# MLPs of a two-layer trunk, first product, chunks 5 to 8: block products accumulated in PSUM, front products adjacent, and A12 by B21 in halves from chunk 6 on

## The chip, the cores and the metric

One core of a Trainium2 chip runs the whole program. The metric is the device time of one execution in microseconds (us), here the median of three runs. PE is TensorE (matmuls), PEld its weight loads, DVE is VectorE, ACT is ScalarE, POOL is GpSimd; SP is the engine whose queue issues nearly all DMAs of this kernel. Every engine works through its own instructions strictly in the order in which they stand in the program, and waits on semaphores for the others.

## The reference

A trunk of two layers on 1024 tokens of width 1024 in float32. Each layer has a mixer, an MLP and a gated projection of a side input p. The change touches the MLPs only:

```python
hn = rms_norm(h, ln_mlp[layer])
h = h + jnp.square(jax.nn.relu(hn @ w_mlp1[layer])) @ w_mlp2[layer]
gate = jax.nn.sigmoid(rms_norm(h, ln_ple[layer]) @ w_ple_gate[layer])
h = h + (p[layer] @ w_ple_proj[layer]) * gate
```

w_mlp1 is 1024 x 4096, w_mlp2 is 4096 x 1024. The "first product" is hn @ w_mlp1.

## The kernel before

**Precision.** Every float32 operand is split into a high part (ACT copies it to the type fp32r) and a low part (DVE subtracts), and mm3 makes three matmuls of each pair: high by high, high by low, low by high.

**The first product** is computed transposed, hidden features on the partitions, in NCH = 8 chunks of 512 hidden features (the code counts them 0 to 7, the text 1 to 8). Each chunk is a 2 x 2 block product (A the weights, B the normed activations, split by 512 of the contraction and by 512 tokens) and is done after Strassen and Winograd with seven block products in place of eight. A block product (product, L335) has two output tiles of 128 x 512, one PSUM bank each, and 24 matmuls of 512 columns. front (L419) makes the first two, A11 by B11 and A12 by B21, accumulated in one pair of banks: after the first ACT copies the running value out as u, after the second it makes g11 = relu^2. rest (L432) makes the other five: (A11-A21) by T3, copied out as v; S1-A11 by T2, added to u, and u to v, on DVE; A22 by T4, on top of the first in its banks, giving g21; S1 by T1, giving g22; and (A12-S2) by B22, on top of that, giving g12. T1 to T4 are sums of the activations' blocks. After each, DVE adds what is in PSUM to u or v, and ACT takes relu and square.

**Halves.** From chunk 3 on (HALVED) the last of these, A12-S2 by B22, is itself done with seven products of half size (halved, L375): 42 matmuls of 256 columns in place of 24 of 512. Their activation parts are made once (halves, L355) and held in the buffers of the pool tmp (tag t, four buffers) and two others. p16 and p57 are two further PSUM banks for its sums.

**Results.** Seven arrays are saved to DRAM per chunk (save, L410), the second product's own operands: gd[0] from g12, gd[1] g22, gd[2] g21, gd[3] and gd[4] from g22 and g21 less v, gd[5] from v = g11 + g12, and gd[6] g21 - g11.

**The second product** follows at once (product2, L570), seven products of 16 steps; each step loads a tile of such an array (graw), splits it, and gives PE 12 matmuls of 512 columns. Its weights come through tiles keep and raw. Early on, split_p (L649) loads p in four tiles through the pool tmp, transposes them on DVE and splits them.

**Buffers and order.** The tiles of the region have one buffer each, named by tag: u of chunk c lies in c0, c1 or c2, c3 (even or odd c), g11 in c4, c5 or c6, c7, g12, g21, g22 in c8 to c13. v lies in two buffers of the pool small. The second product's raw tiles go round c0, c1, c4, c5, its split tiles round c2, c6, c8, c10 and their neighbours, except the first four, which take the buffers of B21:

```python
raws, ring = itertools.cycle((0, 1, 4, 5)), itertools.cycle((2, 6, 8, 10))
```

A tile's next writer waits until its last reader is done, a save's DMA included. The weights' blocks go through 8 raw buffers and 12 split ones. PSUM has 8 banks, four tags with two each, taken in turn (mm_ps, L164). Fronts run two chunks ahead of their rests (those of chunks 3 and 4 are kept in DRAM meanwhile). The code is written in this order, but the order in which an engine's instructions stand is decided by the framework's scheduler, which places them by its own timeline. Each DMA of SP signals one of eight semaphores in turn, and waits until the DMA before it on the same semaphore has landed.

## Time and profile before

| | us |
|---|---|
| median of 3 runs | 2466.21 (2464.63 to 2469.31) |
| the profiled execution | 2463.99 |
| its span, first to last instruction | 2462.3 |
| first save of a chunk, MLP 1 and MLP 2 | 535.1 and 1803.1 |
| last save of a chunk, MLP 1 and MLP 2 | 794.3 and 2058.6 |

The profile is one execution on the chip. A row of the timeline has the start, the length, the engine, the line of the program, the operation, output <- input by the program's names, and how many such instructions stand in a row; a bracket at the end is the engine's idle time before it and what ended that. A row of groups has the count, the busy time, the mean length in ns, and the idle time before. Matmuls overlap in the pipeline, so a matmul's length is more than the time from one start to the next. For DMAs, the time to landing is from the issue on the queue to the semaphore's update. In the lines of this profile, L226 and L225 are split, L284 is tt, L324 is load, L412 is save, L658 the transpose of p.

### The profile page before, as it was taken

How to read it: one execution, taken by the hardware profiler on the slowest of the kernel's cores; microseconds unless marked ns; L12 is line 12 of the kernel's file. 1: busy time of each engine (PE TensorE's matmuls, PEld its weight loads, DVE VectorE, ACT ScalarE, POOL GpSimd, SP SyncE). 2: the span in 40 equal slices, each digit the busy share in tenths (PEclk: the TensorE clock that was granted, in tenths of full speed). 3: DMA queues.
4: the chain of work that ended last, by engine and by line, in shares of the span. 5: the costliest groups of instructions: out<-in, count | busy, mean ns of one | idle time of the engine just before them, and what ended most of it. 6: DMA issues, size and time to landing. Idle time of an engine off the chain costs nothing.

```text
span 2462.3 us, 40587 instructions
## 1 busy us (share of the span) xinstructions
PE 2446.6 (99%) x13709; PEld 2105.3 (85%) x13709; DVE 1922.5 (78%) x3806; ACT 1332.3 (54%) x2740; POOL 319.2 (13%) x304
## 2 busy tenths in 40 slices
PE   9999999999999999999999999999999999999999
PEld 7898998888888888888899999988878888888887
DVE  7787766699788888566568888876898788978677
ACT  6554474465555434454366766664655555445543
POOL 0221231000000000000244443342000000000010
PEclk9999999999999999999999999999999999999999
DMA  8385654456557856553347766787456559657772
GB/s 249 114 260 119 172 186 153 141 168 210 190 173 262 269 182 200 186 174 112 116 104 167 163 166 161 195 225 239 141 172 222 178 183 308 227 184 223 231 246 86
DMA packets 555032, 459.12 MB, mean 186 GB/s; under 512 B 248260, under 2 KB 416456, under 8 KB 554824
## 3 DMA queue, kind: packets, MB, share of 16 engines
q1 hardware_dynamic: 524472, 451.28, 59.5%
q10 hardware_dynamic: 29584, 3.68, 1.0%
q8 instruction: 108, 1.77, 0.3%
q0 software_dynamic: 768, 1.57, 0.2%
q14 instruction: 100, 0.82, 0.1%
HBM read 322.04 MB, written 134.37 MB: 185 GB/s over the span
## 4 chain that ended last, share of the span: by engine, by line
PE 94%; DVE 2%; ACT 2%; DMA 2%; issue 1%; POOL 0%; SPq 0%; DVEq 0%; ACTq 0%; POOLq 0%
PE mm L79 83%; PE po L79 3%; PE qk L79 2%; PE aux L79 2%; PE tr L82 1%; DMA a_dram<-lg 0%; DVE w L226 0%; PE aux L82 0%; PE pvn L79 0%; PE pkq L79 0%; PE pst L79 0%; DMA raw<-in_w_mlp_dram 0%; PE pks L79 0%; ACT guv L1697 0%; ACT w L225 0%
## 5 line engine op out<-in xcount | busy, mean ns | idle before, releaser
L79 PE MATMUL mm<-g,w 128*128 128x512 f32 x2592 | 602.9, 394 | 0.4 <-DVE g L226 0.4
L225 ACT CAST w<-raw 128x512 fp32r<-128x512 f32 (+1 forms) x622 | 377.6, 613 | 414.0 <-PE mm L79 339.2
L79 PEld LDWEIGHTS mm<-g,w 128*128 128x128 f32 x2592 | 486.8, 188 | 114.5 <-DVE g L226 0.8
L79 PE MATMUL mm<-hi,w 128*128 128x512 f32 (+1 forms) x1728 | 528.4, 383 | 0.4 <-DVE w L226 0.4
L79 PE MATMUL mm<-w,hi 128*128 128x256 f32 (+2 forms) x2528 | 500.5, 294 | 0.2
L226 DVE TENSOR_TENSOR w<-raw,w 128x512 fp32r<-128x512 f32 (+2 forms) x534 | 362.6, 685 | 128.0 <-ACT w L225 119.9
L79 PEld LDWEIGHTS mm<-w,hi 128*128 128x128 f32 x2528 | 400.4, 188 | 14.1 <-DVE w L226 0.4
L79 PEld LDWEIGHTS mm<-hi,w 128*128 128x128 f32 x1728 | 316.6, 188 | 63.9 <-DVE w L226 0.8
L79 PE MATMUL mm<-w,lo 128*128 128x256 f32 (+2 forms) x1264 | 367.8, 292 | 0.0
L79 PE MATMUL mm<-lo,w 128*128 128x512 f32 (+1 forms) x864 | 329.2, 382 | 0.0
L79 PE MATMUL mm<-t,w 128*128 128x512 f32 x1152 | 274.0, 394 | 0.4 <-DVE t L226 0.2
L79 PEld LDWEIGHTS mm<-t,w 128*128 128x128 f32 x1152 | 216.1, 188 | 51.8 <-DVE t L226 1.1
L79 PEld LDWEIGHTS mm<-w,lo 128*128 128x128 f32 x1264 | 237.6, 188 | 5.4
L79 PEld LDWEIGHTS mm<-lo,w 128*128 128x128 f32 x864 | 162.8, 188 | 31.9
L225 ACT CAST g<-graw 128x512 fp32r<-128x512 f32 x216 | 132.6, 617 | 33.0 <-DMA graw<-gd 25.3
L226 DVE TENSOR_TENSOR g<-graw,g 128x512 fp32r<-128x512 f32 x216 | 147.5, 686 | 3.7 <-ACT g L225 3.6
L1134 ACT ACTIVATE lg<-lg,nm 128x128 f32<-128x128 f32 (+7 forms) x128 | 99.2, 775 | 74.7 <-DVE nm L1131 72.8
L266 POOL TENSOR_TENSOR r<-ms,mhalf 128x4 f32<-128x4 f32 x12 | 12.5, 1043 | 940.4 <-DVE ms L264 914.1
L226 POOL TENSOR_TENSOR w<-raw,w 128x512 fp32r<-128x512 f32 (+1 forms) x88 | 113.7, 1313 | 132.1 <-ACT w L225 98.9
L350 ACT ACTIVATE g<-g 128x512 f32<-128x512 f32 x96 | 60.2, 630 | 64.7 <-DVE g L284 64.6
L1131 DVE CUSTOM_DVE_ANT_0 lg<-qk,al 128x512 f32<-128x512 f32 (+3 forms) x128 | 72.3, 568 | 25.7 <-PE qk L79 22.4
L79 PE MATMUL mm<-ohi,w 128*128 128x512 f32 x256 | 85.9, 400 | 0.2 <-DVE aT L1348 0.2
(353 smaller groups left out, 3689.7 us busy)
## 6 DMA issues: line engine op xcount, KB each, us to landing
raw<-in_w_mlp_dram SPq DMA_DIRECT2D x352, 256.0 KB, 3.3
graw<-gd SPq DMA_DIRECT2D x224, 256.0 KB, 2.8
gd<-g SPq DMA_DIRECT2D x192, 256.0 KB, 3.2
raw<-in_w_ple_gate_dram SPq DMA_DIRECT2D x76, 256.0 KB, 3.7
acc<-h_dram SPq DMA_DIRECT2D x64, 256.0 KB, 4.3
keep<-in_w_mlp_dram SPq DMA_DIRECT2D x64, 256.0 KB, 5.1
raw<-in_w_in_e_dram SPq DMA_DIRECT2D x60, 256.0 KB, 3.7
h_dram<-acc SPq DMA_DIRECT2D x48, 256.0 KB, 2.2
```

The source lines that it names most:

```text
L79: self._next(self.engine.matmul(*a, **k))
L82: self._next(self.engine.transpose(*a, **k))
L225: self.nc.scalar.copy(hi, src)
L226: (lo_engine or self.nc.vector).tensor_tensor(lo, src, f32(hi), ALU.subtract)
L266: nc.gpsimd.tensor_tensor(r, ms, self.mhalf[:, 0:4], ALU.pow)
L350: nc.scalar.activation(g, src, AF.Relu)
L1131: nc.vector.tensor_tensor_reduce(out=lg[:, k0:k1], in0=ps[:, : k1 - k0], in1=al[:, u0 + k0 : u0 + k1], scale=-1.0, scalar=3.0e38 if c == 0 ...
L1134: nc.scalar.activation(lg[:, :n], lg[:, :n], AF.Exp, bias=nm[:, r, nch - 1 : nch], scale=-1.0, accum_out=me.sums[:, b, r : r + 1])
```

## The change

Chunks 5 to 8 (CHAINED = 4, counted from 0) go through a new function, chain, in place of front and rest:

- A11 by B11 is made in a pair of banks and copied out by ACT as g11. A12 by B21 goes into banks of its own (ps2), and DVE adds it to g11. Then S1-A11 by T2, (A11-A21) by T3 and A22 by T4 follow in the first pair of banks, one on top of another; ACT copies u out after the first, g22 after the second, and after the third g21 is made straight from PSUM. S1 by T1 and (A12-S2) by B22 go on as before.
- The front products of a chunk stand right ahead of its other products, not two chunks earlier.
- All four chunks use c0, c1 for u, c4, c5 for g11, c8, c9 for g12, c10, c11 for g21, and the two buffers of v for g22; u is overwritten with g11 + g12 and saved. The last subtractions and the saves of gd[3] and gd[4] move into the next chunk (close), behind its A12 by B21.
- In chunk 5 halves is called for B21 too (ys2, kept in c2, c3, c6, c7, c12, c13 and in B21's own buffers), and from chunk 6 on A12 by B21 is done by halved: 42 matmuls of 256 columns in place of 24 of 512.

```diff
@@ -27,6 +27,7 @@
 RB = 8
 AHEAD = 7
 HALVED = 2
+CHAINED = 4
 WB = 12
 EARLY = 3000
 LAG = 3
@@ -352,28 +353,37 @@
 
         L, R = slice(0, 256), slice(256, 512)
 
-        def halves():
-
-            y = {(1, 1): [[z[:, L] for z in b22[k]] for k in (0, 1)], (2, 1): [[z[:, L] for z in b22[k]] for k in (2, 3)],
-                 (2, 2): [[z[:, R] for z in b22[k]] for k in (2, 3)], 1: [[z[:, R] for z in b22[k]] for k in (0, 1)]}
-            y2, y3 = ([self.tp.tile([P, 2, 256], F32R, tag="t", name=self.nm("y")) for _ in range(2)] for _ in range(2))
-            y4 = [self.sp.tile([P, 2, 256], F32R, tag=t, name=self.nm("y"), bufs=1) for t in ("sqs1", "rb1")]
-            y.update({n: [[z[:, k] for z in parts] for k in range(2)] for n, parts in ((2, y2), (3, y3), (4, y4))})
+        def halves(b, spare):
+
+            y = {(1, 1): [[z[:, L] for z in b[k]] for k in (0, 1)], (2, 1): [[z[:, L] for z in b[k]] for k in (2, 3)],
+                 (2, 2): [[z[:, R] for z in b[k]] for k in (2, 3)], 1: [[z[:, R] for z in b[k]] for k in (0, 1)]}
+            parts = spare()
+            y.update({n: [[z[:, k] for z in parts[n]] for k in range(2)] for n in parts})
             for k in range(2):
                 d, e = (self.raw(1, HT)[:, 0] for _ in range(2))
-                tt(d, *(f32(z) for z in b22[k]), ALU.add)
-                tt(e, *(f32(z) for z in b22[2 + k]), ALU.add)
+                tt(d, *(f32(z) for z in b[k]), ALU.add)
+                tt(e, *(f32(z) for z in b[2 + k]), ALU.add)
                 tt(d[:, L], d[:, R], d[:, L], ALU.subtract)
                 tt(d[:, R], e[:, R], d[:, R], ALU.subtract)
                 tt(e[:, R], e[:, R], d[:, L], ALU.subtract)
                 tt(e[:, L], e[:, L], e[:, R], ALU.subtract)
                 self.split(d[:, L], *y[1][k])
-                for src, parts in ((e[:, R], y2), (d[:, R], y3), (e[:, L], y4)):
-                    self.split(src, *(z[:, k] for z in parts))
+                for src, n in ((e[:, R], 2), (d[:, R], 3), (e[:, L], 4)):
+                    self.split(src, *(z[:, k] for z in parts[n]))
                 yield y
 
+        def small():
+            y = {n: [self.tp.tile([P, 2, 256], F32R, tag="t", name=self.nm("y")) for _ in range(2)] for n in (2, 3)}
+            y[4] = [self.sp.tile([P, 2, 256], F32R, tag=t, name=self.nm("y"), bufs=1) for t in ("sqs1", "rb1")]
+            return y
+
+        def freed():
+            return {n: [self.slot(f"c{o + i}", [P, 2, 256], F32R, "y") for i in range(2)] for n, o in ((2, 2), (3, 6), (4, 12))}
+
         def halved(raws, y, ps, u):
 
+            new = not ps
+            ps = ps or [self.mm_ps() for _ in range(2)]
             a0, a1 = raws
             lo, hi = slice(0, P), slice(P, 2 * P)
             s12, s4 = self.raw(2, 256), self.raw(2, P)
@@ -392,8 +402,8 @@
             u0, u1 = u
             sub(p16, a0, lo, y[1, 1], True)
             tt(u0[:, L], u0[:, L], p16, ALU.add)
-            sub(ps[0][:, L], a1, lo, y[2, 1])
-            sub(ps[1][:, L], a1, hi, y[4])
+            sub(ps[0][:, L], a1, lo, y[2, 1], new)
+            sub(ps[1][:, L], a1, hi, y[4], new)
             sub(p5, s12, lo, y[1], True)
             for z in u:
                 tt(z[:, R], z[:, R], p5, ALU.add)
@@ -401,11 +411,12 @@
             sub(p7, a0, hi, y[3], True)
             u1 = u1.rearrange("p (h t) -> p h t", h=2)
             tt(u1, u1, p7.unsqueeze(1).to_broadcast([P, 2, 256]), ALU.add)
-            sub(ps[0][:, R], s4, slice(0, P), y[2, 2])
+            sub(ps[0][:, R], s4, slice(0, P), y[2, 2], new)
             sub(p16, s12, hi, y[2])
             tt(u0[:, R], u0[:, R], p16, ALU.add)
             tt(u1, u1, p16.unsqueeze(1).to_broadcast([P, 2, 256]), ALU.add)
             marks.append(self.pe.mark)
+            return ps
 
         def save(n, c, g):
             for i in range(2):
@@ -450,7 +461,7 @@
                 tt(u[i], u[i], ps6[i], ALU.add)
                 tt(v[i], u[i], v[i], ALU.add)
             if c == HALVED:
-                made = halves()
+                made = halves(b22, small)
                 next(made)
             product(a22, t4, ps)
             for i in range(2):
@@ -487,6 +498,74 @@
                 tt(g21[i], g21[i], v[i], ALU.subtract)
             save(4, c, g22)
             save(5, c, g21)
+
+
+        def chain(c, close):
+
+            u, g11, g12, g21 = (tiles((f"c{o}", f"c{o + 1}"), "g") for o in (0, 4, 8, 10))
+            g22 = [self.sp.tile([P, HT], F32, tag=f"{n}0", name=self.nm("v"), bufs=1) for n in ("sqs", "rb")]
+            ps = product(block(c, 0, 0), b11)
+            for i in range(2):
+                nc.scalar.copy(g11[i], ps[i])
+            a12 = block(c, 0, 1)
+            if c > CHAINED:
+                ps2 = halved(a12, ys2, None, g11)
+            else:
+                ps2 = product(a12, b21)
+            close()
+            s1 = self.slot("B", [P, 2, 2, 256], F32, "s1")
+            s1 = [s1[:, i] for i in range(2)]
+            a21, a22, a11 = block(c, 1, 0), block(c, 1, 1), block(c, 0, 0)
+            for i in range(2):
+                tt(s1[i], a21[i], a22[i], ALU.add)
+                tt(a21[i], a11[i], a21[i], ALU.subtract)
+                tt(a11[i], s1[i], a11[i], ALU.subtract)
+            for i in range(2):
+                cols = L if i and c > CHAINED else slice(0, HT)
+                tt(g11[i][:, cols], g11[i][:, cols], ps2[i][:, cols], ALU.add)
+                relu2(g11[i], g11[i])
+            product(a11, t2, ps)
+            for i in range(2):
+                nc.scalar.copy(u[i], ps[i])
+            if c == CHAINED:
+                made = halves(b21, freed)
+                next(made)
+            product(a21, t3, ps)
+            for i in range(2):
+                nc.scalar.copy(g22[i], ps[i])
+            if c == CHAINED:
+                ys2.update(next(made))
+            product(a22, t4, ps)
+            for i in range(2):
+                relu2(g21[i], ps[i])
+                tt(g11[i], g21[i], g11[i], ALU.subtract)
+            save(3, c, g21)
+            save(7, c, g11)
+            ps = product(s1, t1)
+            for i in range(2):
+                tt(g22[i], g22[i], ps[i], ALU.add)
+                relu2(g22[i], g22[i])
+            save(2, c, g22)
+            a12 = block(c, 0, 1)
+            for i in range(2):
+                tt(a12[i], a12[i], a11[i], ALU.subtract)
+            halved(a12, ys, ps, u)
+            for i in range(2):
+                tt(g12[i], u[i], ps[i], ALU.add)
+                relu2(g12[i], g12[i])
+            save(1, c, g12)
+            for i in range(2):
+                tt(u[i], g11[i], g12[i], ALU.add)
+            save(6, c, u)
+
+            def close():
+                for i in range(2):
+                    tt(g22[i], g22[i], u[i], ALU.subtract)
+                    tt(g21[i], g21[i], u[i], ALU.subtract)
+                save(4, c, g22)
+                save(5, c, g21)
+
+            return close
 
 
         away = {c: self.dp.tile([4, P, HT], F32, name=self.nm("away")) for c in (2, 3)}
@@ -512,15 +591,17 @@
         front(2, away[2])
         self.pe.floor = None
         front(3, away[3])
-        t4, t1, b22, ys = [], [], [], {}
+        t4, t1, b22, ys, ys2 = [], [], [], {}, {}
         t3, t2, make_t4, make_t1 = operands()
-        for c in range(NCH):
+        for c in range(CHAINED):
             rest(c)
             if c + 2 in away:
                 for i, t in enumerate(itertools.chain(*places(c + 2))):
                     nc.sync.dma_start(t, away[c + 2][i])
-            elif c + 2 < NCH:
-                front(c + 2)
+        close = lambda: None
+        for c in range(CHAINED, NCH):
+            close = chain(c, close)
+        close()
 
 
         accs = [self.slot(f"A{i}", [P, 4, HT], F32, "acc") for i in range(4)]
```

The scheduler orders anew from chunk 3 to the beginning of the second product; PE has 108 matmuls more in all. Three places.

**SP at the hand-over from the first product to the second, first MLP.** In names such as gd_5714, 5707 to 5714 are gd[0] of the eight chunks, 5754 is gd[5], 5738 gd[3] and 5746 gd[4] of the last one; graw_8826 before and graw_8960 now are the second product's first tile, in c0. Before:

```order
L412 DMA gd_5721<-g_8240 128x512
L324 DMA keep_8820<-in_w_mlp_dram 128x512
L324 DMA graw_8826<-gd_5707 128x512
L412 DMA gd_5713<-g_8235 128x512
L412 DMA gd_5753<-v_8241 128x512
L412 DMA gd_5713<-g_8236 128x512
```

The first tile was loaded between saves of chunk 7. Now, with g_8528 and g_8529 the last chunk's u in c0 and c1, and t_9352, t_9361 and t_9370 the tiles of p:

```order
L738 DMA t_9352<-in_p_dram 32x16x32 x4
L738 DMA t_9361<-in_p_dram 32x16x32 x4
L423 DMA gd_5714<-g_8532 128x512
L738 DMA t_9370<-in_p_dram 32x16x32
L423 DMA gd_5754<-g_8528 128x512
L325 DMA graw_9008<-gd_5708 128x512
L423 DMA gd_5714<-g_8533 128x512
L738 DMA t_9370<-in_p_dram 32x16x32
L423 DMA gd_5738<-v_8536 128x512
L423 DMA gd_5746<-g_8534 128x512
L423 DMA gd_5754<-g_8529 128x512
L325 DMA graw_8960<-gd_5707 128x512
```

The first tile's load has moved behind the last chunk's saves of u and behind loads of p. DVE at the same place, now (t_9353 is the transposed first tile of p, g_8533 is g12's second tile, g_8528 on the left is u):

```order
L285 TENSOR_TENSOR g_8532<-g_8528,mm_8807 128x512
L227 TENSOR_TENSOR w_9077<-keep_9074,w_9076 128x512
L285 TENSOR_TENSOR g_8529<-g_8529,mm_8869 128x512
L739 STREAM_TRANSPOSE t_9353<-t_9352 128x512
L285 TENSOR_TENSOR g_8533<-g_8529,mm_8808 128x512
L285 TENSOR_TENSOR g_8528<-g_8530,g_8532 128x512
```

The sum that makes u stands behind the transpose; before, all such sums of the last chunk stood ahead of it.

**PE at the same hand-over.** mm_8735 and mm_8673 before, and mm_8870 now, belong to the last chunk's halves (128x256); hi_8828 and hi_8962 are the high part of the second product's first tile. Before:

```order
L79 MATMUL mm_8673<-hi_6346,w_8732 128x256
L79 MATMUL mm_8816<-hi_8828,w_8822 128x512
L79 MATMUL mm_8816<-lo_8829,w_8822 128x512
L79 MATMUL mm_8735<-y_6822,w_8727 128x256
L79 MATMUL mm_8735<-y_6823,w_8727 128x256
L79 MATMUL mm_8735<-y_6822,w_8728 128x256
```

Now:

```order
L80 MATMUL mm_8870<-y_6824,w_8853 128x256
L80 MATMUL mm_8870<-y_6825,w_8853 128x256
L80 MATMUL mm_8870<-y_6824,w_8854 128x256
L80 MATMUL mm_8950<-hi_8962,w_8956 128x512
L80 MATMUL mm_8951<-hi_8962,w_8956 128x512
L80 MATMUL mm_8952<-hi_8962,w_8956 128x512
```

Before, matmuls of the second product stood among the last ones of the halves; now the second product begins behind all of them.

**PE inside chunk 6.** mm_7744 is the first bank of the chain; w_7887 and w_7888 are of S1-A11 (by T2), w_7917 and w_7918 of A11-A21 (by T3):

```order
L80 MATMUL mm_7744<-t_6153,w_7887 128x512
L80 MATMUL mm_7744<-t_6154,w_7887 128x512
L80 MATMUL mm_7744<-t_6153,w_7888 128x512
L80 MATMUL mm_7744<-hi_6128,w_7917 128x512
L80 MATMUL mm_7744<-lo_6129,w_7917 128x512
```

The next product into the bank follows the one before it directly, with ACT's copy of u between them; before, these two products had banks of their own.

## Prediction

> **What bounds the kernel now.** I read the page's totals first, then its chain of work, then stretches of time inside the stage that changes.
>
> ```profile
> span 2462.3 us, 40587 instructions
> PE 2446.6 (99%) x13709; PEld 2105.3 (85%) x13709; DVE 1922.5 (78%) x3806; ACT 1332.3 (54%) x2740; POOL 319.2 (13%) x304
> PE 94%; DVE 2%; ACT 2%; DMA 2%; issue 1%; POOL 0%; SPq 0%; DVEq 0%; ACTq 0%; POOLq 0%
> ```
>
> PE is busy all the time and is 94% of the chain that ended last. So a saved matmul is saved time, and any new wait of PE is lost time, nanosecond for nanosecond. Does PE wait anywhere in the stage that changes? The view of stretches answers (length; then busy us of PE, PEld, DVE, ACT, POOL with instruction counts; clock; DMA share; GB/s):
>
> ```profile
> 740.00:760.00 20.00, 20.00 (x109) 17.18 (x108) 17.77 (x34) 11.56 (x20) 0.00 (x0) 1.00 0.40 138
> 760.00:780.00 20.00, 20.00 (x106) 17.00 (x105) 17.90 (x33) 13.63 (x26) 0.00 (x0) 1.00 0.88 308
> 780.00:800.00 20.00, 20.00 (x91) 16.42 (x90) 16.61 (x28) 10.45 (x19) 0.00 (x0) 1.00 1.05 346
> 2025.00:2045.00 20.00, 20.00 (x106) 17.02 (x105) 18.00 (x33) 13.01 (x24) 0.00 (x0) 1.00 0.92 317
> ```
>
> These cover the last chunk of the first product and the hand-over to the second one (about 783 us in the first MLP, 2047 us in the second). PE never rests; DVE is 86 to 90% busy, and at the hand-over the DMA engines are full (1.05). There is no idle time to win here, only work to remove.
>
> **What the change removes.** A matmul's pitch comes from runs of one shape in the timeline (start, length, engine, line, count):
>
> ```profile
> 753.91 1.56 PE L79 MATMUL mm<-y,w 128*128 128x256 f32 x12
> 758.33 14.08 PE L79 MATMUL mm<-t,w 128*128 128x512 f32 x60
> 782.51 0.87 PE L79 MATMUL mm<-y,w 128*128 128x256 f32 x6
> 790.84 0.40 PE L79 MATMUL mm<-hi,w 128*128 128x512 f32 x1
> 791.27 0.69 DVE L226 TENSOR_TENSOR w<-keep,w 128x512 fp32r<-128x512 f32 x1 [1.63 <-PE mm L79]
> ```
>
> Without the last one's length, (14.08-0.39)/59 = 0.232 us for 512 columns, and (1.56-0.28)/11 and (0.87-0.28)/5 = 0.117 us for 256. A12 by B21 was 24 matmuls of 512 columns, 5.57 us; in halves it is 42 of 256, 4.91 us. Three chunks in each of two MLPs: 6 x 0.65 = **3.9 us less**. The last two rows give the time from a matmul's start to a waiting engine's start: 0.43 us.
>
> The additions that disappear from DVE are worth nothing by themselves: DVE is not the bound, and in return come those of the second halved product and, in chunk 5, the making of B21's halves. Counted in the order, DVE has 40 instructions more per MLP and ACT 22; at 0.6 us apart, 56 to 68 DVE rows per chunk fill 31 to 36 of its 38 us. PE's work covers that; if the cover goes, it shows as the waits below. SP's number of DMAs stays, POOL's queue is untouched. The front products' loads move behind the saves of the chunk before; their weights are still asked for most of a chunk ahead, so I cost that at nothing.
>
> **What it adds at the hand-over.** Before, odd chunks kept u and g11 in c2, c3, c6, c7, so the last chunk left c0, c1, c4, c5 alone, and product2, which loads its first four raw tiles there, had its first load out at 758.8 us, some 20 us ahead of need:
>
> ```profile
> L324 SPq DMA_DIRECT2D graw<-gd x13: 319/429/594, 758.8 to 800.0; - x13
> ```
>
> Now every chained chunk uses c0, c1 for u and c4, c5 for g11. The load into c0 can only go out when the last chunk's u has been made from g12 and its save has landed. The order shows it: on SP that load stands behind the save, and on PE product2's first matmul stands right behind the last one of the halves, with nothing between. Moreover SP puts the load of p's first tile ahead of u's save, and DVE puts that tile's transpose ahead of the sum that makes u; that tile sits in a buffer that the halves of B22 hold until the last chunk's last two products. The durations:
>
> ```profile
> L657 SPq DMA_DIRECT2D t<-in_p_dram x16: 312/462/1045, 780.0 to 814.8; - x16
> DMA to landing us min/median/max: 4.3/5.2/6.8
> ...
> L658 DVE STREAM_TRANSPOSE t<-t x8: 702/708/712, 793.7 to 2082.4; 128x512 f32<-128x512 f32 x8
> ...
> L284 DVE TENSOR_TENSOR g<-u,mm 128x512 f32<-128x512 f32 x8 | 5.5, 682 | 1.3 <-PE mm L79 1.3
> ...
> L226 DVE TENSOR_TENSOR lo<-graw,hi 128x512 fp32r<-128x512 f32 x4 | 2.8, 688 | 0.7 <-ACT hi L225 0.7
> ...
> L225 ACT CAST hi<-graw 128x512 fp32r<-128x512 f32 x4 | 2.5, 618 | 2.2 <-DMA graw<-gd 2.1
> ...
> graw<-gd SPq DMA_DIRECT2D x224, 256.0 KB, 2.8
> gd<-g SPq DMA_DIRECT2D x192, 256.0 KB, 3.2
> ```
>
> Saves and loads of 256 KB land after 3.2 and 2.8 us (medians over the kernel). With the DMA full at the hand-over it was more: the next two rows are those of the saves between 785 and 796 us and of the loads between 780 and 815 us.
>
> ```profile
> DMA to landing us min/median/max: 4.4/4.7/5.3
> ...
> DMA to landing us min/median/max: 4.5/5.5/6.6
> ```
>
> The waits stretch SP's issues out, so the DMA will be less full; I take 4.0 and 4.2 us, between the two. Now the walk, from T, when the matmul that frees p's buffer has been issued; after it PE has six matmuls of 256 columns left, 0.7 us:
> - four loads of p issued at 0.46 us each, the last at T+1.6, landed at T+6.8;
> - transpose 0.7, the addition ahead of u 0.7, u 0.7: T+8.9;
> - u's save lands at T+13.1 (a load of p that the same semaphore counts, issued at T+7.6, lands at T+12.8, in its shadow);
> - the load into c0 lands at T+17.4, ACT casts it, PE starts at T+18.2: **a wait of 17.5 us**;
> - the clock comes back slow, see below: the first twelve matmuls take up to 5.2 us instead of 2.8;
> - the second tile's low part stands on DVE behind the transpose of p's third tile, whose last load is issued at T+16.8: landed T+22.0, transposed, low part at T+23.4. PE would have asked at about T+22, or T+24 at the slow clock.
>
> Behind the waiting matmul stands all of product2 on PE; behind the waiting load stand, on SP, the last saves of arrays 4 and 5 and the loads of the next tiles, which is why the second tile is late as well. Together, PE is through its second tile at T+26 to T+27 where it would have been at T+6.3: about **20.5 us per MLP, 41 in all**. With the shortest landings (2.0 us for saves and loads is the least of the kernel, in the row below, and 4.3 for p) the same walk ends 16 us late, with the longest (5.5, 6.6 and 6.8) 24 us.
>
> ```profile
> DMA to landing us min/median/max: 2.0/3.0/6.7
> ```
>
> **The clock.** This trace shows one longer rest of PE, near its start, and what follows:
>
> ```profile
> 7.93 1.85 PE L82 MATMUL aux<-ident,x 128*128 128x128 f32 x8 [2.39 <-DMA x<-in_x_dram]
> 10.42 0.63 PE L79 MATMUL mm<-lo,w 128*128 128x512 f32 x1
> 10.85 0.63 PE L79 MATMUL mm<-hi,w 128*128 128x512 f32 x1
> ...
> 9.00:12.00 3.00, 3.00 (x11) 2.47 (x10) 2.33 (x5) 3.00 (x8) 0.00 (x0) 0.55 1.09 366
> 12.00:15.00 3.00, 3.00 (x21) 2.62 (x20) 2.97 (x5) 3.00 (x9) 0.00 (x0) 1.00 1.09 363
> ```
>
> After sparse work and a rest of 2.4 us the granted clock was 0.55 for 3 us and the pitch 0.43 us. A wait of 17 us should do the same, 12 x 0.2 = 2.4 us at most, half of it hidden under the wait for the second tile; I took 1.3. The Trainium skill's page "TensorE: Matmul & The Clock Gate", Part 1, says that PE falls to half rate after an idle window of about 3.4 us and needs as long a busy one to recover; by that rule the price would be, as an estimate, 1.7 to 3.4 us per restart before anything hides it, and the trace agrees with one window.
>
> **What it adds inside the chunks.** The running sums stay in PSUM, but ACT copies them out between two products into one bank, so PE waits for ACT:
>
> ```profile
> L445 ACT COPY v<-mm x32: 577/587/591, 522.7 to 2031.6; 128x512 f32<-128x512 f32 x32
> ```
>
> From the last matmul's start, 0.43 to ACT, 0.59 for the copy and 0.1 back is 1.1 us. In chunk 6 the next product into the bank follows at once (0.23 us): 0.9 us lost. In chunks 7 and 8 six matmuls of 256 columns stand between (0.93 us): 0.2. Also, the first product's copy out waits for the old g11, read last by the previous chunk's u: from that chunk's last matmul 0.43 + seven DVE rows of 0.4 to 0.7 + the copy, some 5.4 us, against 8 x 0.232 + 24 x 0.117 = 4.7 us of PE's work: 0.7 lost in chunks 7 and 8, none in chunk 6, where 5.4 us of work stand there. With ACT's queue about 1 us for each of these chunks, 0.5 for chunk 5: 3.5 per MLP, **7 us**. The ends: nothing, if the order's slack covers it, and 0.9 us at each of four products into one bank, 3.6 x 4 x 2 = 29 us. I take 7, near the lower end, because most banks have 3 to 5 us of other products between.
> The Trainium skill's page "PSUM — Partial Sum Buffer", section on bank collisions, says that ACT's read and PE's write of one bank must not overlap, and that nothing arbitrates; without the rule this term could be 0, with it 7; no run here shows a collision.
>
> **Sum.** Against the profiled execution's own 2463.99 us (span 2462.3 and 1.7 around it; the median of the runs shown is 2466.21, 0.1% above): 2463.99 - 3.9 + 41 + 7 = **2508 us**, 1.8% slower.
>
> **Rivals.**
> 1. *p does not gate.* Its loads land early enough, so only the chain of u remains: 0.4 to DVE, 0.4, 0.7, two activations of 0.63 and u's 0.7 make T+3.5; save 3.2, load 2.8, cast 0.6: T+10.1, a wait of 9.4 us, 19 for both: 2464 - 3.9 + 19 + 7 = 2486; up to 2491 with the slow clock. Against it: the loads' shortest landing is 4.3 us and they are issued after T.
> 2. *The chunks wait much more*: DVE, at 31 to 36 of 38 us, falls behind, and the in-bank copies cost their upper end, 29 instead of 7: 2530. For it: DVE's fill; against: PE never waited for DVE at 90% before.
> 3. *Faster.* The hand-over is covered after all: u's save lands while PE still has work, and only the 3.9 us are left: 2460. It decides at a hand-over wait of under 1.9 us per MLP. Against it: u cannot be made before the last matmuls but six, and save, load and cast take 4.6 us at their very shortest.
> 4. *Same*: waits of about 2 us per MLP, by the same mechanism.
>
> **Chances.** Forecast 0.70 (2494 to 2522), rival 1 0.12, rival 2 0.13, faster 0.03, same 0.02 (the bound is 0.2%, 5 us, about what a measurement of this kernel can tell from none). The range must reach into rivals 1 and 2: 2486 to 2530.
>
> **What would show it.** In the changed kernel's profile: matmuls up by 108; one PE wait of 15 to 20 us in each MLP right ahead of product2, ended by ACT's cast of a graw tile, which itself ends a wait for its DMA; a second wait of 1 to 3 us one tile later, ended by DVE; a granted clock of about 0.5 for some 3 us behind it; waits of PE of about 1 us or less in chunks 6 to 8, ended by ACT. The forecast is wrong if PE goes from the halves into product2 without a gap, or if the waits inside chunks together exceed those at the hand-over.

## The result, and the profile after

| | us |
|---|---|
| changed kernel, median of 4 runs | 2510.07 (2507.47 to 2511.83) |
| kernel before on the same chip, median of 4 | 2465.88 (2464.63 to 2469.31) |
| ratio, 95% interval | 1.0177 (1.0164 to 1.0189) |
| profiled execution after, and its span | 2510.51, 2508.8 |

The change makes the kernel 44 us slower, 1.8%. The page of the changed kernel, totals and the chain of work that ended last:

```profile
PE 2450.7 (98%) x13817; PEld 2110.2 (84%) x13817; DVE 1947.9 (78%) x3886; ACT 1354.3 (54%) x2784; POOL 320.4 (13%) x304
PE 89%; DVE 5%; DMA 3%; issue 1%; ACT 1%; SPq 0%; POOL 0%; DVEq 0%; ACTq 0%; POOLq 0%
```

PE's share of the chain fell from 94 to 89%; DVE and DMA took its place. What it waited for in the stages that changed, costliest first (line, waited for, us in total, times, longest; rows of other stages left out):

```profile
PE mm L80 <- ACT hi L226: 27.4, 2, 14.0
PE mm L80 <- ACT g L509: 7.9, 7, 2.9
PE mm L80 <- DVE w L227: 2.6, 5, 0.8
PE mm L80 <- DVE g L285: 1.9, 3, 1.1
PE mm L80 <- ACT g L529: 1.4, 2, 0.7
```

The first row is the hand-over from the first to the second product, one stop per MLP; L509 is the copy of g11 out of PSUM, L529 that of u; L285 is tt. The hand-over of the first MLP in the timeline, a selection of rows:

```profile
785.83 1.58 PE L80 MATMUL mm<-y,w 128*128 128x256 f32 x12
786.62 4.05 SPq L738 DMA_DIRECT2D t<-in_p_dram  x8
790.53 0.70 DVE L739 STREAM_TRANSPOSE t<-t 128x512 f32<-128x512 f32 x1
791.73 0.67 DVE L285 TENSOR_TENSOR g<-g,g 128x512 f32<-128x512 f32 x1
792.43 0.34 SPq L423 DMA_DIRECT2D gd<-g  x1
792.82 0.43 SPq L325 DMA_DIRECT2D graw<-gd  x1
793.35 0.40 SPq L423 DMA_DIRECT2D gd<-g  x1
793.79 0.43 SPq L738 DMA_DIRECT2D t<-in_p_dram  x1
794.32 0.60 SPq L423 DMA_DIRECT2D gd<-v  x1
795.01 0.90 SPq L423 DMA_DIRECT2D gd<-g  x2
796.00 1.72 SPq L325 DMA_DIRECT2D graw<-gd  x2
800.75 1.25 ACT L226 CAST hi<-graw 128x512 fp32r<-128x512 f32 x2 [4.12 <-DMA graw<-gd]
801.42 2.08 PE L80 MATMUL mm<-hi,w 128*128 128x512 f32 x4 [14.01 <-ACT hi L226]
...
803.29 0.63 PE L80 MATMUL mm<-lo,w 128*128 128x512 f32 x1
803.72 0.63 PE L80 MATMUL mm<-hi,w 128*128 128x512 f32 x1
...
807.96 0.39 PE L80 MATMUL mm<-lo,w 128*128 128x512 f32 x1
```

Read from the last products of the halves (first row): p's loads go out, its first tile is transposed; u is summed (791.73) and saved (792.43). The load into c0 needs that save, and by the trace's record of its semaphore the save landed 2.1 us after its issue, at 794.55. But on SP's queue, which works in order, six more issues stand ahead of the load (another tile's load, four saves of the last chunk, a load of p), with no pause between two of them longer than 0.1 us, so it goes out only at 796.00, 3.6 us after the save was issued. It lands 4.7 us later, is cast, and PE starts. Then the first fourteen matmuls come 0.43 us or more apart instead of 0.232: 801.42 to 807.96 is 6.54 us for 16 matmuls that take 3.71 at the full clock, so 2.8 us more.

To compare many kernels I sum, over all matmul records of a stretch, the distance from one start to the next less the undisturbed pitch (0.232 us for 512 columns, 0.118 for 256). This counts waits and slow clock together. "Chunks" is chunks 5 to 8 of both MLPs, "hand-over" the end of the first product and the first block tiles of the second one. The kernel before has 0.3 and 0.0; the changed one 17.4 and 33.0. A figure somewhat under 0 means none: the pitch taken is a little high. With the 3.9 us of removed matmuls, -3.9 + 17.4 + 33.0 = 46.5 us, which is the difference of the two spans (2508.8 - 2462.3 = 46.5). So on balance nothing of the loss lies elsewhere; in the runs below the two sides of this sum differ by up to 3.4 us.

### The profile page after: what moved, and what is told of

It reads as the page before. It is cut to its first block, busy times and chain, and to the rows that moved or that the text cites. A ratio compares the mean times of both kernels' runs of the same rounds, so it can differ in the third digit from the quotient of the medians.

```text
span 2508.8 us, 40972 instructions
## 1 busy us (share of the span) xinstructions
PE 2450.7 (98%) x13817; PEld 2110.2 (84%) x13817; DVE 1947.9 (78%) x3886; ACT 1354.3 (54%) x2784; POOL 320.4 (13%) x304
## 4 chain that ended last, share of the span: by engine, by line
PE 89%; DVE 5%; DMA 3%; issue 1%; ACT 1%; SPq 0%; POOL 0%; DVEq 0%; ACTq 0%; POOLq 0%
PE mm L80 79%; PE po L80 3%; PE qk L80 2%; PE aux L80 2%; DVE w L227 1%; DMA raw<-in_w_mlp_dram 1%; PE tr L83 1%; DVE g L285 1%; DVE raw L285 0%; DMA spill<-early 0%; DMA graw<-gd 0%; DMA aT<-a_dram 0%; PE pkq L80 0%; PE pvn L80 0%; DMA acc<-h_dram 0%
## 5 line engine op out<-in xcount | busy, mean ns | idle before, releaser
L226 ACT CAST w<-raw 128x512 fp32r<-128x512 f32 x634 | 382.2, 611 | 429.2 <-PE mm L80 348.9
L80 PE MATMUL mm<-hi,w 128*128 128x512 f32 (+1 forms) x1728 | 525.6, 380 | 31.3 <-ACT hi L226 27.4
L80 PE MATMUL mm<-t,w 128*128 128x512 f32 x1152 | 278.2, 395 | 10.2 <-ACT g L509 7.9
L226 ACT CAST g<-graw 128x512 fp32r<-128x512 f32 x216 | 132.7, 617 | 26.9 <-PE mm L80 10.2
L80 PE MATMUL mm<-ahi,w 128*128 128x512 f32 x256 | 84.3, 400 | 1.2 <-ACT ahi L1825 1.2
```

The lines of the kernel that those rows point to most:

```text
L80: self._next(self.engine.matmul(*a, **k))
L226: self.nc.scalar.copy(hi, src)
```

## The experiments

All are timed against the kernel before on the same chip. Pauses in us, from the profiled execution of each.

| run | what it is | median, us | ratio (95%) | pauses in chunks | at hand-over |
|---|---|---|---|---|---|
| | the change | 2510.07 | 1.0177 (1.0164 to 1.0189) | 17.4 | 33.0 |
| ring | change, free tiles first in the second product | 2499.63 | 1.0131 (1.0115 to 1.0148) | 16.9 | 21.0 |
| ring2 | ring, u's pair last | 2493.17 | 1.0105 (1.0091 to 1.0119) | 15.7 | 14.5 |
| five | ring2, u and g11 over five tiles | 2480.28 | 1.0055 (1.0041 to 1.0068) | 7.1 | 10.5 |
| five_free | five, no tile with a late save early on | 2470.42 | 1.0020 (1.0011 to 1.0028) | 6.8 | 0.4 |
| p_later | change, p written later | 2511.34 | 1.0175 (1.0160 to 1.0190) | 19.2 | 32.1 |
| p_gated | change, p's loads tied to later matmuls | 2507.67 | 1.0169 (1.0155 to 1.0184) | 18.3 | 31.4 |
| nohalf | change, A12 by B21 whole | 2506.67 | 1.0160 (1.0145 to 1.0175) | 8.0 | 32.3 |
| nohalf_alt | nohalf, u and g11 in alternate pairs | 2481.48 | 1.0057 (1.0042 to 1.0072) | -0.6 | 17.9 |
| alt_ring2 | nohalf_alt, u's pair last | 2477.02 | 1.0041 (1.0028 to 1.0054) | -0.6 | 12.9 |
| alt_free | alt_ring2, no tile with a late save early on | 2468.24 | 1.0006 (0.9998 to 1.0015) | -0.6 | 2.0 |
| before_ring | kernel before, second product's tiles dealt the wrong way | 2482.81 | 1.0066 (1.0051 to 1.0081) | 1.4 | 19.9 |

### Does the stop come from c0, or from what stands around it? (ring)

```diff
-        raws, ring = itertools.cycle((0, 1, 4, 5)), itertools.cycle((2, 6, 8, 10))
+        raws, ring = itertools.cycle((2, 3, 6, 7)), itertools.cycle((0, 4, 8, 10))
```

> The changed kernel, with the buffers of the second product dealt out the other way round: its raw block products are loaded into c2, c3, c6, c7 (which hold the extra operands of the halved A12 by B21 and come free some 25 us before the first product ends), and the split pairs go to c0, c4, c8, c10. Theory 1 (the stop between the two products comes from the first loads waiting for the last chunk's u and g11 to be summed and saved): both stops of 14.0 and 13.4 us go, and with them the slow clock behind them, 33 us by the trace of the changed kernel; 2477 us (2472 to 2483). Theory 2 (p's loads and transposes, or VectorE being behind at the end of the chunk, hold the second product up whichever buffer it loads into): the stop shrinks by less than half, 2495 us or more.

Measured 2499.63: by the bound, the second theory. The waits view says otherwise. Both stops ended by the cast of the first block tile are gone; instead, at the fifth tile:

```profile
PE mm L80 <- DVE g L227: 7.1, 3, 3.4
PE mm L80 <- ACT g L226: 6.9, 2, 4.7
```

It is the first tile that is split into a pair of the ring (g, not hi and lo). PE waits for its high part before the first matmul on it and for its low part behind the fourth, and its pair is now c0, c1: u again. So the mechanism was right and the forecast of its size wrong: with u's pair dealt next, two thirds of the pauses at the hand-over stayed (21.0 of 33.0).

### The same wait at another tile, or ScalarE's order? (ring2)

```diff
-        raws, ring = itertools.cycle((0, 1, 4, 5)), itertools.cycle((2, 6, 8, 10))
+        raws, ring = itertools.cycle((2, 3, 6, 7)), itertools.cycle((4, 8, 10, 0))
```

> As the run ring, whose raw block products went into the free tiles, but with the pair c0, c1 (u) last among the split pairs instead of first: c4, then c8, c10, c0. In ring the stop of 14 us was gone and two shorter ones of 2.4 to 4.9 us stood at the fifth and sixth block tile, the fifth being the first that is split into c0, c1. Theory 1 (those stops are the same wait on u, moved four tiles on): both go, 2484 us (2480 to 2489). Theory 2 (they are ScalarE's order: its cast of a piece of w2 that waits 4.1 us for its load stands ahead of the last activations of the chunk and of the casts of the block tiles, whatever the pair): they stay, 2499 us (2494 to 2502).

Measured 2493.17, between the two. One stop per MLP is left, 4.3 and 6.6 us. Four matmuls on tiles g stand ahead of it in PE's timeline, so it lies within the fifth block tile, which waits for its low part (the expectations here and below count such stops to the sixth tile, that of alt_free with the pair c8, c9). In the first MLP of ring2:

```profile
796.09 0.62 ACT L226 CAST w<-keep 128x512 fp32r<-128x512 f32 x1 [4.42 <-DMA keep<-in_w_mlp_dram]
798.65 0.69 DVE L285 TENSOR_TENSOR g<-g,g 128x512 f32<-128x512 f32 x1 [1.22 <-ACT g L352]
801.05 0.68 DVE L227 TENSOR_TENSOR g<-graw,g 128x512 fp32r<-128x512 f32 x1
801.79 1.65 PE L80 MATMUL mm<-g,w 128*128 128x512 f32 x3 [4.33 <-DVE g L227]
```

The fifth tile's pair is c4, c5 here, the last chunk's g11. Its second half is read last by the sum that makes u's second half (798.65). That sum waits for the chunk's last activation, and on ACT this stands behind a cast that waits 4.4 us for a piece of w2. Three more rows of DVE follow, then the low part (801.05). So a late tile and ScalarE's order meet, and this run doesn't tell the two theories apart; alt_free below does.

### Does p stand in the way? (p_later, p_gated)

p_later moves the call:

```diff
-        pT = self.split_p(p)
         ps = product2(6)
+        pT = self.split_p(p)
         for q in range(4):
```

> The changed kernel with p's loads, transposes and splits written one block product later in the second product (after its second group of products instead of its first), buffers as they were. Theory 1 as the prediction put it (p stands ahead of u and its save): the stop falls from 14.0 to about 9.4 us in each MLP, 9 us together, 2501 us (2497 to 2504). Theory 2 (in the profile of the changed kernel p's first tiles landed soon enough to hold back nothing but a microsecond or two; the chain sum, save, load, split does it alone): 2508 us (2505 to 2511), stops over 12 us.

2511.34 us, but it says nothing on p. Eight loads of p go out in its timeline 0.8 us after the row of the last products begins (788.20), as in the changed kernel:

```profile
788.99 4.05 SPq L738 DMA_DIRECT2D t<-in_p_dram  x8
```

The scheduler put them at the same place on the queue, although the call is written one product later. p_gated ties p's loads to a matmul of the second product instead, with the helper that the block loads use:

```diff
-        pT = self.split_p(p)
+        pT = self.split_p(p, marks[-AHEAD])
...
-                nc.sync.dma_start(raw[...], p[...])
+                self.pe.behind(nc.sync.dma_start(raw[...], p[...]), mark)
```

> The changed kernel with p's loads tied to the tenth matmul group of the second product's first part, as the block loads around it are tied to theirs, so that p's loads, transposes and splits leave the stretch between the two products (in the run p_later they had stayed there, since both buffers and queue let them). Theory 1, of the prediction (p stands ahead of u's sum, save and reload): the stop falls from 14.0 and 13.4 to about 9.4 us in each MLP, 2501 us. Theory 2 (by the profile of the changed kernel one transpose of 0.70 us stands ahead of u's sum and nothing else of p delays the chain): the stop falls by 0.5 to 1.2 us per MLP, 2508 us (2506 to 2511).

Measured 2507.67; the two stops together 26.6 us instead of 27.4. The timeline of p_gated, with no load of p in it:

```profile
789.07 1.58 PE L80 MATMUL mm<-y,w 128*128 128x256 f32 x12
794.48 0.68 DVE L285 TENSOR_TENSOR g<-g,g 128x512 f32<-128x512 f32 x1
798.83 1.00 SPq L325 DMA_DIRECT2D graw<-gd  x1
803.23 0.62 ACT L226 CAST hi<-graw 128x512 fp32r<-128x512 f32 x1 [3.98 <-DMA graw<-gd]
803.90 0.80 PE L80 MATMUL mm<-hi,w 128*128 128x512 f32 x1 [13.26 <-ACT hi L226]
```

From the first row's start, u's sum begins 5.4 us later (5.9 in the changed kernel), the load goes out after 9.8 (10.2), the cast starts after 14.2 (14.9). Without p the stop is 0.7 us shorter in the first MLP and hardly shorter in the second (13.4 in both runs); the second theory holds. The stop is the chain of sum, save, place in SP's queue, load and cast by itself: here the save landed 2.0 us after its issue (797.19), and the load went out 1.6 us after that, again behind other issues.

### The halving, and the single pairs (nohalf, nohalf_alt)

nohalf takes the whole product of A12 by B21 in chunks 6 to 8 too (the condition `c > CHAINED` is never true) and doesn't make B21's halves. nohalf_alt then deals u and g11 to alternate pairs, as the kernel before does:

```diff
-            u, g11, g12, g21 = (tiles((f"c{o}", f"c{o + 1}"), "g") for o in (0, 4, 8, 10))
+            u, g11, g12, g21 = (tiles((f"c{o}", f"c{o + 1}"), "g") for o in (2 * (c % 2), 4 + 2 * (c % 2), 8, 10))
```

> The changed kernel without its second part: A12 by B21 stays whole in chunks 6 to 8, so the six spare tiles c2, c3, c6, c7, c12, c13 stay empty; u and g11 still have one buffer pair each. TensorE work rises by 3.9 us. Theory 1 (the waits inside chunks, 19 us by the trace, come from VectorE and ScalarE being behind, which the halving feeds with additions and splits): they fall to about 6, 2501 us (2497 to 2506), stops at the hand-over as before. Theory 2 (the waits come from the single buffer of g11, whatever the load): they stay, 2514 us (2511 to 2517).

> As the run without the halved A12 by B21, and with u and g11 in alternate pairs (c0, c1 and c4, c5 in chunks 5 and 7; c2, c3 and c6, c7 in chunks 6 and 8), which leaves the accumulation in PSUM and the order as the only part of the change. Theory 1 (accumulating costs nothing of itself; all of the loss is in the buffers and in the load of the halving): stops at the hand-over under 1 us and waits inside chunks under 3, 2466 us (2463 to 2471), that of the kernel before within 0.2%. Theory 2 (the order itself, with the copies out of PSUM between two products of one accumulation, costs): 2475 us or more.

nohalf: 2506.67, just outside the first theory's range; pauses in chunks fell from 17.4 to 8.0, near the 6 expected, and some 3 us of its span (2506.0 - 2462.3 = 43.7 against 8.0 + 32.3) lie outside these stages. 2.0 of them lie ahead of the first save of a chunk (at 537.0 us, against 535.1 in the kernel before), where the change has no part; the rest stays unexplained. The kind of wait changed. nohalf in the chunks of the first MLP:

```profile
PE mm L80 <- ACT g L529: 2.6, 3, 1.3
PE mm L80 <- ACT g L509: 0.8, 1, 0.8
```

where the changed kernel has, in the same stretch:

```profile
PE mm L80 <- ACT g L509: 5.1, 3, 2.9
```

beside 0.9 for sums and 0.7 for u's copy (L529). Without the halves the copy of g11 is in time and u's copy is a little late. With alternate pairs no wait is left inside the chunks at all, though the sums still accumulate in PSUM and ACT still copies between two products into one bank: accumulation costs nothing here. nohalf_alt missed its 2466 us (2481.48) by the hand-over: the second product's first ring pair, c2, c3, is the last chunk's u in this layout.

### How the copy of g11 comes to be late

Chunk 8 of the first MLP in the changed kernel's timeline:

```profile
752.98 0.63 ACT L352 ACTIVATE g<-g 128x512 f32<-128x512 f32 x1
755.03 0.68 DVE L227 TENSOR_TENSOR w<-raw,w 128x512 fp32r<-128x512 f32 x1
756.23 0.68 DVE L285 TENSOR_TENSOR g<-g,g 128x512 f32<-128x512 f32 x1
756.95 0.59 ACT L509 COPY g<-mm 128x512 f32<-128x512 f32 x1
757.59 2.59 PE L80 MATMUL mm<-t,w 128*128 128x512 f32 x10 [2.88 <-ACT g L509]
```

Chunk 7's g12 is ready when its second activation ends (753.61). Its sum with the old g11 (the row g from g and g) starts only at 756.23, behind five other rows of DVE, operands of the coming products among them (one is shown). ACT may overwrite the old g11 only then, and the bank that the next product needs is free after the copy. Three things meet: one pair of g11, a halved product that needs more of DVE, and a shorter time until PE asks.

### Can the whole change be had without the waits? (five, five_free, alt_ring2, alt_free)

five uses one idle tile, d0, as a fifth, and turns the dealing round by chunks (its last chunk has g11 in c0, c1, so the split pairs follow as c0, c8, c10, c4):

```diff
-            u, g11, g12, g21 = (tiles((f"c{o}", f"c{o + 1}"), "g") for o in (0, 4, 8, 10))
+            a, b, d, e, s = five
+            five[:] = s, a, b, d, e
+            u, g11, g12, g21 = (tiles(t, "g") for t in ((d, e), (a, b), ("c8", "c9"), ("c10", "c11")))
...
+        five = ["c4", "c5", "c0", "c1", "d0"]
```

> The whole change with the halved products, second product as in ring2, and u and g11 dealt out over five tiles (c0, c1, c4, c5 and the idle d0) instead of four: each chunk's g11 takes the spare tile and the first tile of the old g11, its u the second of the old g11 and the first of the old u. Theory 1 (the waits inside chunks are those of ScalarE's copies for the one pair of g11 and of u): the waits inside chunks fall from 23 us in ring to about 8, and the time to that of ring2 less 15 us; at best 2469 us (2464 to 2480). Theory 2 (they are VectorE and ScalarE being behind with the additions and splits of two halved products in a chunk): less than 5 us below ring2.

> As the run nohalf_alt (A12 by B21 whole, u and g11 in alternate pairs), with the split pairs of the second product in the order c6, c8, c10, c2, so that the last chunk's u comes last instead of first. nohalf_alt had no waits inside chunks and two stops of 2.9 to 3.8 us per MLP behind the fourth block tile. Theory 1 (accumulating in PSUM costs nothing of itself, the rest of the loss is the wait on u): the stops go, 2467 us (2464 to 2471), the time of the kernel before within 0.2%. Theory 2 (ScalarE's order holds the tiles back): 2480 us (2476 to 2484).

five: 2480.28, just above the first theory's range and 13 us below ring2, and pauses in chunks fell from 15.7 to 7.1: the first theory's mechanism, though a stop at the hand-over kept it from 2469. That stop lies within the fifth tile, whose pair, c0, c1, is the last chunk's g11. alt_ring2: 2477.02, in the second theory's range; one stop of some 4.5 us per MLP, within the fifth tile again. What ScalarE does there, in alt_ring2:

```profile
785.08 0.32 SPq L423 DMA_DIRECT2D gd<-g  x1
789.77 0.62 ACT L226 CAST g<-graw 128x512 fp32r<-128x512 f32 x1 [4.40 <-issue]
791.34 0.63 ACT L352 ACTIVATE g<-g 128x512 f32<-128x512 f32 x1
795.08 0.68 DVE L227 TENSOR_TENSOR g<-graw,g 128x512 fp32r<-128x512 f32 x1
795.82 1.46 PE L80 MATMUL mm<-g,w 128*128 128x512 f32 x4 [4.42 <-DVE g L227]
```

A cast, by its place that of the sixth tile into c8, waits 4.4 us. The view names no releaser, but by the trace's record of its semaphore the save issued at 785.08 landed at 789.70, just before the cast starts; that it is g12's is inferred from the pair. The chunk's last activation (791.34) stands behind that cast on ACT, the sum that reads g11's second half last stands behind the activation, and the fifth tile's low part (795.08) goes into that half: c6, c7 are g11 here. So the last two runs give the fifth tile a pair that is free early (c4, c5 and c6, c7), the first tiles only places without a late save, and the second product's own u a pair that isn't free early:

```diff
-        raws, ring = itertools.cycle((0, 1, 4, 5)), itertools.cycle((6, 8, 10, 2))
+        raws, ring = itertools.cycle((0, 1, 12, 13)), itertools.cycle((4, 6, 8, 10))
-        u = [ub[:, 0], ub[:, 1], *tiles(("c12", "c13"), "u")]
+        u = [ub[:, 0], ub[:, 1], *tiles(("c2", "c3"), "u")]
```

That is alt_free against alt_ring2. five_free likewise has raws 2, 5, 12, 13, ring 6, 0, 8, 10 and u in c3, c4.

> As alt_ring2 (A12 by B21 whole, u and g11 in alternate pairs), with the second product's first tiles all where nothing of the last chunk is saved late: raw block products in c0, c1, c12, c13, split pairs in the order c4, c6, c8, c10, and the second product's own u in c2, c3 in place of c12, c13. In alt_ring2 one stop of 4.6 and 4.8 us was left at the sixth block tile, whose pair c8, c9 waits for g12's save: ScalarE's cast stands ahead of the last activations of the chunk. Theory 1 (buffers are all that is left): the stops go, 2466 us (2463 to 2470), within 0.2% of the kernel before. Theory 2 (the second product is held up by something else at that place): 2475 us or more.

> As the run five (whole change, u and g11 over five tiles), with raw block products in c2, c5, c12, c13, split pairs in the order c6, c0, c8, c10, and the second product's own u in c3, c4. Theory 1: the stops of 4.1 and 2.3 us at the sixth block tile go, and what is left is 10 us of small waits inside chunks against 3.9 us of TensorE work saved: 2473 us (2470 to 2477), still above the kernel before by 0.1 to 0.4%. Theory 2 (the stop stands elsewhere then): 2480 us.

Both as expected: 2468.24 (1.0006, with 1 inside the interval) and 2470.42 (1.0020). In alt_free ACT still waits for its piece of w2, and PE hardly at all:

```profile
789.53 0.62 ACT L226 CAST w<-keep 128x512 fp32r<-128x512 f32 x1 [4.07 <-DMA keep<-in_w_mlp_dram]
794.43 5.82 PE L80 MATMUL mm<-g,w 128*128 128x512 f32 x23 [0.24 <-DVE g L227]
```

The longest wait left there is 1.2 us, in the second MLP. That settles what ring2 left open: ScalarE's wait is no bound of its own; it costs PE only where a tile that PE needs soon waits for what stands behind it on ACT. Which of the three edits did it (raw tiles, pairs, u) no run separates; what is left lies within the sixth tile, whose pair c6, c7 is g11, and that fits the pairs. And the removed work is real. The row of busy times of five_free's page:

```profile
PE 2443.1 (99%) x13817; PEld 2105.1 (85%) x13817; DVE 1946.3 (79%) x3886; ACT 1350.8 (55%) x2784; POOL 320.9 (13%) x304
```

and of alt_free's, which has the whole product:

```profile
PE 2446.9 (99%) x13709; PEld 2104.8 (85%) x13709; DVE 1901.7 (77%) x3774; ACT 1336.7 (54%) x2756; POOL 321.0 (13%) x304
```

The halves save 3.8 us of PE (2446.9 - 2443.1) and give back 6.8 in pauses inside the chunks. No version tried beats the kernel before.

### The stop in the kernel before (before_ring)

> The kernel before, with nothing changed but the dealing of the second product's buffers: raw block products in c2, c3, c6, c7 (the pairs of u and g11 that its last chunk uses) and split pairs in c0, c4, c8, c10. Theory 1 (the seamless hand-over of the kernel before rests on the alternate pairs, and the stop needs neither accumulation nor halving): a stop appears in each MLP. u is not saved here, so the first load waits only for g12's sum, some 3.5 us after the last matmul that it needs, then 4.7 us of load and 0.7 of cast: about 8 us and 1 to 2 of slow clock each, 2486 us (2480 to 2494). Theory 2 (it is the order of the chunks' tail): 2467 us, no stop.

The edit is that of ring, made in the kernel before. Measured 2482.81. Its waits view has a row that the kernel before doesn't have:

```profile
PE mm L79 <- ACT hi L225: 13.4, 2, 6.8
```

Two stops of 6.6 to 6.8 us, and 3 us each of slow clock and small pauses behind them: neither the accumulation nor the halved A12 by B21 is needed for the stop, only a first tile that the last chunk has just used. It is half as long as in the changed kernel: u isn't saved here, and the first load goes out (782.85 us) as soon as the sum that reads u has ended (782.84).

## Why the prediction was right, and where its steps were not

The time was forecast as 2508 and came as 2510; the stop at the hand-over was named as the bulk, with its cause, its place and its releaser, and all that was confirmed by taking the cause away (alt_free, five_free) and by putting it into the old kernel (before_ring). But two terms were off in opposite ways, one by 8 us and one by 10; that the total came within 2 us was luck. Of the signs that the prediction named, the matmuls, the stop's place and releaser and the half clock came; the stops were shorter than 15 us, the second wait one tile later was missing, and waits inside the chunks reached 2.9 us, not about 1.

| term | forecast | measured |
|---|---|---|
| A12 by B21 in halves | -3.9 | -3.8 |
| hand-over, both MLPs | 41 | 33 |
| inside chunks | 7 | 17.4 |

- **Matmuls removed.** As forecast: 13817 against 13709, 3.8 us.
- **The wait at the hand-over: 17.5 forecast, 14.0 and 13.4 measured.** The step that failed is that p gates. With T where p's first load goes out (786.6), p's tile was to be landed at T+6.8 and u made at T+8.9; its four loads landed 2.2 us after their issues, the last at T+3.6, DVE took up the transpose at T+3.9 without having idled for it, and u was done at T+5.8. The landing times taken (5.2) came from the kernel before, whose DMA was full there (share 1.05); after the change it was not. That this is the reason is inferred; no run varies it alone:

```profile
785.00:788.00 3.00, 2.41 (x21) 2.21 (x19) 2.91 (x7) 2.10 (x4) 0.00 (x0) 1.00 0.65 226
788.00:801.00 13.00, 0.00 (x0) 0.00 (x0) 9.81 (x17) 4.58 (x8) 0.00 (x0) 0.59 0.88 248
```

In the rest of the walk, the 3.6 us from u's save to the load look like the 4.2 taken, but are another thing: 2.1 us of landing and 1.5 us of SP's queue, for which the walk has no term. Load 4.7 (4.3) and cast 0.6 were as taken.
- **The second tile's wait** didn't show. The low part that the forecast had at T+23.4, that is 810, is there by 806.4 (a row of DVE at 805.78), while PE at the slow clock started the first tile's last matmul only at 806.28.
- **The clock** cost 2.8 and 2.5 us (16 matmuls from 2089.01 to 2095.21 in the second MLP), not 1.3: no other wait hid part of it, and it lasted longer than at the program's start (the last section shows why). The estimate of 1.7 to 3.4 us per restart that the prediction set beside its own term holds both.
- **Rival 1** (p does not gate) was right in its premise and wrong in its price: 9.4 us of wait, against 13.3 in p_gated. It let u be made at T+3.5, with nothing on DVE ahead, and took the kernel's median landings; with p away u was done 5.3 us after the same point, the load went out 3.7 us later (save landed after 2.0, then SP's queue) and took 4.4.
- **Inside the chunks: 7 forecast, 17.4 measured**, a term mis-sized in its step on the copy of g11. That step gave 0.7 us in chunks 7 and 8 and none in chunk 6, from seven DVE rows between the chunk's last matmul and u. In the first MLP the next product came 0.9, 1.7 and 3.0 us late in chunks 6, 7 and 8, because operands of other products stand on DVE ahead of u's sum (shown for chunk 8 above). Waits for u's copy came to 1.4 in all, less than the 2.6 forecast; waits of PE for operands and sums of DVE itself, up to 4.5 in all, had no term. nohalf and five show the cause from both sides: less work on DVE, or a free tile, and the wait goes.
- **Rival 2** (29 us inside chunks) overshot: its in-bank copies at each product cost nothing where a second pair was there (nohalf_alt). Its other half, DVE falling behind, did show: it is what made the copy of g11 late, though in the kernel before PE hardly waits for DVE in these chunks. The page "PSUM — Partial Sum Buffer" of the Trainium skill (bank collisions) was cited for the order of ACT's read and PE's write of a bank; no run here shows a collision.

## What to carry to other kernels

Before two loops share tiles, list for the hand-over which tiles the first one frees last, and by which engine; a tile that is summed, saved and then loaded again puts the whole chain (14 us here) in front of PE, and moving it a few tiles on only moves the wait. Look also at what stands ahead of the load on its queue, and ahead of the last activations on ACT: here both cost time after the data was there. The space that a new operand takes (six tiles for B21's halves) is paid where those tiles used to be the second buffer: here 3.9 us of matmuls were bought with 50 us of waits. When terms come from a trace in which a resource was full, ask whether it will still be full once PE has stopped.

## What the hardware showed unexpectedly

After the stop the half clock lasted longer than at the program's start. The clock doesn't seem to count from the restart: in this trace its changes stand on a grid. It fell at 790.36 and 2080.60 and came back at 807.42 and 2094.25, and all distances between these four are whole multiples of 3.41 us (5, 373 and 4 of them). Windows of that grid, two pieces (windows: length, busy times, clock, DMA share, GB/s):

```profile
800.60:804.01 3.41, 2.59 (x6) 2.11 (x7) 1.32 (x2) 1.65 (x3) 0.00 (x0) 0.50 1.12 350
804.01:807.42 3.41, 3.41 (x9) 2.64 (x9) 2.97 (x5) 2.48 (x5) 0.00 (x0) 0.50 1.05 260
807.42:810.83 3.41, 3.41 (x16) 2.77 (x16) 2.45 (x5) 1.86 (x3) 0.00 (x0) 1.00 0.85 261
...
2090.84:2094.25 3.41, 3.41 (x9) 2.64 (x8) 1.79 (x3) 1.44 (x3) 0.00 (x0) 0.50 1.01 314
2094.25:2097.66 3.41, 3.41 (x16) 2.79 (x15) 2.69 (x6) 2.63 (x6) 0.00 (x0) 1.00 1.00 238
```

PE restarted at 801.42 and 2089.01, inside a window. The full clock came only behind the first window in which PE was busy throughout, so 6.0 and 5.2 us after the restart: the rest of one window and the whole of the next. Behind the stops of nohalf and before_ring it came 2.9 to 6.5 us after the restart; once, in nohalf, 2.9 us of one window were enough, so how much of a window is needed stays open. The Trainium skill's page "TensorE: Matmul & The Clock Gate", Part 1, gives such a window of about 3.4 us, which runs on whatever the kernel does, and one busy window for the return to full rate; the windows above agree.
